# Layer 1's attention on one Trainium2 core: the heads taken two by two, TensorE's order written out

## The chip, the core and the metric

The program runs on one core of a Trainium2 chip, in one launch. The core has TensorE (matrix multiplies, and transposes by a multiply with the identity), VectorE (DVE), ScalarE (ACT), GpSimd (POOL) and SyncE (SP, which here only starts DMA transfers). Each takes its own instructions in order and waits on semaphores for the others. Multiplies write PSUM, of which the program uses eight banks of 128 partitions x 512 fp32; everything else lives in SBUF. The metric is the device time of one execution in microseconds (us), the median over the runs.

## The reference, cut to what matters

Two layers over 256 tokens of width 1024: retention and a dense SwiGLU, then chunked attention and a top-2-of-8 SwiGLU with expert weights of 352 MB. The change is in layer 1's attention: 16 heads of 64 dimensions, each 64-token chunk against its own and the eight chunks before it, with a bias.

```
def one_chunk(args):
    c, q_c = args
    ...
    s = jnp.einsum('bihd,bjhd->bhij', q_c, k_band).astype(jnp.float32) + bias
    ...
    a = jax.nn.softmax(s, axis=-1).astype(v_band.dtype)
    return jnp.einsum('bhij,bjhd->bihd', a, v_band)
o = lax.map(one_chunk, (jnp.arange(nc), q))
...
return o @ w_o
```

## The kernel before

All weights stream from HBM in units of 1 MB. The class `Stream` loads a unit into a raw buffer (SP), and splits it into a high half (a cast on ACT, L157) and a low half (a subtraction on DVE, L158), into a pair of buffers `whi`, `wlo`; five pairs are in rotation from the middle of the attention on. Each product is three multiplies (high by high, high by low, low by high) in fp32r, for which a multiply stands once in the trace. The attention's own small products (scores, transposes, values) are plain fp32, for which each multiply stands twice in the trace, with a weight load each.

In layer 1 the keys `kT` and queries `qT` are kept with 64 dimensions of a head on partitions 0 to 63 (even heads, `par` 0) or 64 to 127 (odd heads, `par` 1). The loop of 19 steps takes one head a step:

- `score(n)`: the scores of head n in one PSUM bank `sc`, two multiplies (256 columns L946, 128 columns L947), each of them 64 rows by 128 columns of the array; then on DVE the bias is added into an SBUF tile `s` and the maxima are taken, and ACT takes the exponentials (L960, L963).
- a piece of filling work for TensorE: in steps 0 to 7 half of a projection `kqps` (24 multiplies of 256 columns), in steps 8 to 17 half a unit of the output projection `y` (`out1`, 6 multiplies of 512 columns, L414 to L418).
- `turn(n-2)`: three transposes into the bank `at` (L974), copied to SBUF by ACT (L977).
- `values(n-3)`: six multiplies into the bank `ao` (L987 to L989; with the odd head four DVE scalings by the sum's reciprocal). Each second step `att_oT` transposes a finished pair (`otr`, L1042), which ACT and DVE split into `ht`, the operand of `out1`.

The banks `sc`, `at`, `ao`, `otr` and `kqps` come from one ring of four; `y` has four of its own. In this loop nothing is ordered by hand: a scheduler places the instructions of each engine, by program order as priority and by readiness in its own plan. Behind the loop the order of TensorE, ACT, DVE and SP is by hand (`order`), through the experts to the end.

Of the kernel before, what the change touches and what calls it, by code (L numbers as in the profile page):

```python
# [9 lines left out]
F32 = mybir.dt.float32  # L10
# [7 lines left out]
P = 128  # L18
T = 256
# [40 lines left out]
PC = 1  # L60
PM = 2
RE = 1
# [21 lines left out]
C_ID, C_TRI, C_IOTA, C_INV, C_DEC = 0, 128, 256, 384, 385  # L84
C_END = C_DEC + HEADS * T
LINE = 16
M = 96
E_X, E_Y, E_END = 0, 8, 64
C_TILE = 400
EDGE = 56  # L90

# [127 lines left out]
def trunk(ctx: ExitStack, tc: tile.TileContext, a, out):  # L219
    nc = tc.nc  # L220
    base = ctx.enter_context(tc.tile_pool(name="base", bufs=1))
# [10 lines left out]

    edge = ctx.enter_context(tc.tile_pool(name="edge", bufs=1, side="right"))
    edge.tile([P, EDGE], F32, name="edge")
    cst = base.tile([P, C_TILE], F32, name="cst")[:, :C_DEC]
    ext = base.tile([P, E_END], F32, name="ext")
    ones = base.tile([P, P], F32, name="ones")
    nhalf = base.tile([P, LINE], F32, name="nhalf")[:, :1]
    wr = base.tile([P, KC, NE], F32, name="wr")
    wrs = base.tile([P, KC, 2 * NE], F32R, name="wrs")  # L240
    gain2 = base.tile([P, 2 * D], F32, name="gain2")
# [60 lines left out]
    st = Stream(nc, units, raws, pairs)  # L302
# [17 lines left out]
    def bank(name):  # L320
        return ring.tile([P, NF], F32, name=name, tag="ring")
# [4 lines left out]
    def t512(name):  # L326
        return tmps[-1].tile([P, NF], F32, name=name, tag="t")

    def s1(name, w=1, dt=F32):
        return small.tile([P, w], dt, name=name, tag=f"s{w}{dt}")  # L330
# [31 lines left out]
    def split_bank(hi, lo, b):  # L362
        nc.scalar.copy(hi, b)  # L363
        nc.vector.tensor_tensor(lo, b, hi.bitcast(F32), op=OP.subtract)  # L364
# [40 lines left out]
    def down(ys, us, xs, first, last, mid=None, at=2):  # L405
        k = 0
        n = sum(u[1][0].shape[1] for u in us)
        for _, (wh, wl) in us:
            for c in range(wh.shape[1]):
                if mid and k == at:  # L410
                    mid()
                for nb in range(2):
                    f = slice(nb * NF, (nb + 1) * NF)
                    nc.tensor.matmul(ys[nb], xs[0][:, k, :], wh[:, c, f], start=first and k == 0, stop=False)  # L414
                    nc.tensor.matmul(ys[nb], xs[0][:, k, :], wl[:, c, f], start=False, stop=False)  # L415
                for nb in range(2):
                    f = slice(nb * NF, (nb + 1) * NF)
                    nc.tensor.matmul(ys[nb], xs[1][:, k, :], wh[:, c, f], start=False, stop=last and k == n - 1)  # L418
                k += 1
# [11 lines left out]
    def hp(n=HP):  # L431
        return tc.high_priority(offset=n) if n else ExitStack()
# [6 lines left out]
    pairs1 = [tuple(pp.tile([P, 1024], F32R, name=f"p{j}{i}") for j in ("hi", "lo")) for i in range(8 - NB)]  # L439
# [73 lines left out]
    def take_ht():  # L513
        x = (htr.popleft(), htr.popleft())
        htr.extend(x)
        return x
# [75 lines left out]
    start = tc.manual_schedule(engines={mybir.EngineType.PE, mybir.EngineType.Activation, mybir.EngineType.DVE})  # L592
# [8 lines left out]
    def norm0(tb):  # L601
        r = s1("rstd")
        nc.vector.tensor_tensor(r, ss[tb][:, 0:1], ss[tb][:, 1:2], op=OP.add)
        nc.vector.tensor_scalar(r, r, 1.0 / D, EPS, op0=OP.mult, op1=OP.add)
        nc.gpsimd.tensor_tensor(r, r, nhalf, op=OP.pow)
        scaled(xh[tb], h[:, tb, :], r, gains[0])
        return [transpose4(xh[tb][:, half * NF : (half + 1) * NF], "xtr") for half in range(2)]
# [4 lines left out]
    b = bank("warm")  # L612
# [4 lines left out]
    bs = norm0(0)  # L617
# [8 lines left out]
    bs = norm0(1)  # L626
# [251 lines left out]
    r3 = ExitStack()  # L878
    stacks.append(r3)
    ap_ = r3.enter_context(tc.tile_pool(name="att", bufs=1))  # L880
    ap3 = r3.enter_context(tc.tile_pool(name="att3", bufs=3))
    vsb = ap_.tile([P, 2, D], F32, name="vsb")
    kT = [ap_.tile([P, 4, T], F32, name=f"kT{i}") for i in range(2)]
    qT = [ap_.tile([P, 4, T], F32, name=f"qT{i}") for i in range(2)]
# [4 lines left out]
    def load_bias(pr):  # L889
        b = bias[pr % 2]  # L890
        nc.sync.dma_start(b[64:128, :, :], a["bias_hi"][:, 2 * pr : 2 * pr + 2, :])
        nc.sync.dma_start(b[0:64, :, :192], a["bias_lo"][:, 2 * pr : 2 * pr + 2, :])
# [44 lines left out]
    class Att:  # L937
        def __init__(self):
            self.s, self.e, self.t = {}, {}, {}

        def score(self, hd):
            half, ch, par = hd // 8, (hd % 8) // 2, hd % 2
            rr = slice(par * 64, par * 64 + 64)
            q, k = qT[half][rr, ch, :], kT[half][rr, ch, :]
            b = bank("sc")
            nc.tensor.matmul(b[:, :T], q[:, P:], k, start=True, stop=True)  # L946
            nc.tensor.matmul(b[:, T : T + P], q[:, :P], k[:, :P], start=True, stop=True)  # L947
            bt = bias[(hd // 2) % 2][:, par, :]
            s = ap3.tile([P, T + P], F32, name="s")
            nc.vector.tensor_tensor(s[:, :T], b[:, :T], bt, op=OP.add)  # L950
            nc.vector.tensor_tensor(s[:, T:], b[:, T : T + P], bt[:, P:], op=OP.add)
            if par == 1 and hd // 2 + 2 < 8:
                load_bias(hd // 2 + 2)
            nm = s1("nm", 2)
            nc.vector.tensor_reduce(nm[:, 0:1], s[:, T:], axis=AX.X, op=OP.max)
            nc.vector.tensor_reduce(nm[:, 1:2], s[:, :T], axis=AX.X, op=OP.max)
            nc.vector.tensor_scalar(nm, nm, -1.0, None, op0=OP.mult)
            if par == 0:
                self.sum = s1("esum", 4)
            nc.scalar.activation(  # L960
                s[:, :T], s[:, :T], AF.Exp, bias=nm[:, 1:2], accum_out=self.sum[:, 2 + par : 3 + par]
            )
            nc.scalar.activation(s[:, T:], s[:, T:], AF.Exp, bias=nm[:, 0:1], accum_out=self.sum[:, par : par + 1])  # L963
            self.s[hd] = s
            if par == 1:
                rs = s1("rsum", 4)
                nc.vector.reciprocal(rs, self.sum)
                self.e[hd // 2] = rs
# [31 lines left out]
    att = Att()  # L1000
# [26 lines left out]
    dst, xo, wo, swapped, late = [], [], {}, [], []  # L1027

    def swap_right():
        p1.close()  # L1030
        mw = m0.enter_context(tc.tile_pool(name="more0", bufs=1, side="right"))
        late.extend(mw.tile([P, 2048], F32, name=f"more{i}") for i in range(6))
        swapped.append(True)

    def att_oT(ch):

        if ch % 2 == 0:
            xo.append(take_ht())
        b = bank("otr")[:, :T].rearrange("p (b t) -> p b t", b=2)
        c = ch % 4 * P  # L1040
        for tb in range(2):
            nc.tensor.transpose(b[:, tb, :], dst[ch // 4][tb][:, c : c + P], ident)  # L1042
        f = slice(ch % 2 * 2, ch % 2 * 2 + 2)
        with hp(H1):
            split_bank(xo[-1][0][:, f, :], xo[-1][1][:, f, :], b)

    def out1(ch, tb, n=99):
        if ch not in wo:
            wo[ch] = st.take1()
        k = ch % 2 * 2 + tb  # L1050
        down(y[tb], wo[ch], [x[:, k : k + 1, :] for x in xo[ch // 2]], ch == 0, ch == 7)
        if tb == 1:
            st.done(wo.pop(ch))
            if not swapped and not st.retired:
                swap_right()
            st.pump1(n)

    fill = proj_fill()
    outs = [(0, 0), (0, 1), (1, 0), (1, 1), (2, 0), (2, 1), (3, 0), (3, 1)] + OV[OO][0]
    for n in range(19):  # L1060
        if n < 16:
            att.score(n)
        if n < 8:
            next(fill, None)
        if n == 8:
            for _ in fill:
                pass
            if not RE:
                st.retire(pairs1)
            elif not st.retired:  # L1070
                swap_right()
        for _ in range(PC if n % PM == 0 else 0):
            if late:
                st.raws.append(late.pop(0))
                st.load()
        if n >= 8 and n < 19 and outs[n - 8]:
            out1(*outs[n - 8])
        if 2 <= n <= 17:
            att.turn(n - 2)
        if n >= 3:  # L1080
            if (n - 3) % 8 == 0:
                dst.append([t512("ao0"), t512("ao1")])
            att.values(n - 3, dst[-1])
        if n >= 5 and n % 2:
            att_oT((n - 5) // 2)
    for x in OV[OO][1]:
        out1(*x)
    att_oT(7)
# [530 lines left out]
    with tc.If(over > M):  # L1619
        with ExitStack() as es:  # L1620
            q = es.enter_context(tc.tile_pool(name="ov", bufs=1))
# [67 lines left out]
```

## Time and profile before

| what | value |
|---|---|
| median of 3 runs | 1562.42 us (1562.37 to 1562.57) |
| the profiled execution | 1563.2 us, of which the span of the instructions is 1561.3 us |
| TensorE | busy 1537.8 us, 98% |
| DVE, ACT | 1275.3 us (82%), 1091.5 us (70%) |
| granted TensorE clock | 0.998 of full speed, which is the upper of its two levels (2.4 GHz) |

The profile is of one execution. A busy TensorE means that some multiply was in its pipeline: a 512-column multiply stands with 0.39 us in the trace, but the next starts 0.23 to 0.24 us behind it. Work on TensorE is therefore read from start to start.

### The profile page before, as it was taken

What the parts mean: (1) busy time and instruction counts of PE and PEld (TensorE: products, weight loads), DVE (VectorE), ACT (ScalarE), POOL (GpSimd) and SP (SyncE); (2) the same over time, 40 slices, a digit from 0 to 9 for tenths busy, and PEclk for the clock granted to TensorE, in tenths of its full rate; (3) what the DMA queues carried; (4) which work ended last, traced back from release to release, by engine and by line L of the source; (5) the groups of instructions that cost most, each with busy time, mean ns of one, the idle gap of its engine ahead of it and who ended that gap; (6) DMA issues with size and microseconds to landing.
All of it is one profiled execution on the core that took longest, in us unless ns stands there. A gap on an engine that the chain in (4) does not pass through costs nothing.

```text
span 1561.3 us, 20789 instructions
## 1 busy us (share of the span) xinstructions
PE 1537.8 (98%) x7556; PEld 1290.6 (83%) x7556; DVE 1275.3 (82%) x1617; ACT 1091.5 (70%) x1461; POOL 48.4 (3%) x67
## 2 busy tenths in 40 slices
PE   7999999999999999999999999999999999999997
PEld 5888888888889888888888888888888888888886
DVE  7866675555774779999999999999999999999995
ACT  6545454554754658888878888888888788788774
POOL 1000010000000001000000000000000000000000
PEclk9999999999999999999999999999999999999999
DMA  8854476555463779999999999999999999999850
GB/s 294 286 180 167 162 254 216 187 188 196 149 217 124 267 269 378 412 391 381 378 382 394 381 373 388 366 382 390 373 386 391 375 368 398 380 369 390 310 211 30
DMA packets 206303, 473.56 MB, mean 303 GB/s; under 512 B 9168, under 2 KB 21328, under 8 KB 206192
## 3 DMA queue, kind: packets, MB, share of 16 engines
q1 hardware_dynamic: 202064, 457.87, 79.8%
q0 software_dynamic: 3840, 13.76, 2.4%
q8 instruction: 61, 1.00, 0.2%
q10 hardware_dynamic: 288, 0.52, 0.1%
q14 instruction: 50, 0.41, 0.1%
HBM read 462.16 MB, written 9.96 MB: 302 GB/s over the span
## 4 chain that ended last, share of the span: by engine, by line
PE 98%; ACT 1%; DVE 0%; DMA 0%; issue 0%; SPq 0%; POOL 0%; ACTq 0%; POOLq 0%; DVEq 0%
PE y L414 9%; PE y L415 9%; PE y L418 9%; PE g L333 8%; PE g L334 8%; PE g L335 8%; PE u L333 8%; PE u L335 8%; PE u L334 8%; PE vps L335 1%; PE vps L333 1%; PE vps L334 1%; PE htr L1230 1%; PE kqps L400 1%; PE qkps L401 1%; PE qkps L402 1%
## 5 line engine op out<-in xcount | busy, mean ns | idle before, releaser
L158 DVE TENSOR_TENSOR wlo<-raw,whi 128x512 fp32r<-128x512 f32 (+1 forms) x414 | 375.0, 929 | 109.5 <-ACT whi L157 94.4
L157 ACT CAST whi<-raw 128x512 fp32r<-128x512 f32 (+1 forms) x414 | 329.0, 812 | 139.0 <-PE y L418 49.7
L158 DVE TENSOR_TENSOR wlo<-more,whi 128x1024 fp32r<-128x1024 f32 (+1 forms) x275 | 327.4, 1214 | 26.4 <-ACT whi L157 14.1
L157 ACT CAST whi<-more 128x1024 fp32r<-128x1024 f32 (+1 forms) x275 | 284.6, 1049 | 58.6 <-PE y L418 29.5
L414 PE MATMUL y<-whi,ht 128*128 128x512 f32 x548 | 216.0, 394 | 0.5 <-ACT ht L363 0.5
L415 PE MATMUL y<-wlo,ht 128*128 128x512 f32 x548 | 213.9, 390 | 0.0
L333 PE MATMUL u<-whi,xd 128*128 128x512 f32 x448 | 180.3, 402 | 0.0
L333 PE MATMUL g<-whi,xd 128*128 128x512 f32 x456 | 177.9, 390 | 0.2 <-ACT xd L363 0.2
L335 PE MATMUL g<-whi,xd 128*128 128x512 f32 x456 | 177.9, 390 | 0.0
L334 PE MATMUL g<-wlo,xd 128*128 128x512 f32 x456 | 177.5, 389 | 0.0
L335 PE MATMUL u<-whi,xd 128*128 128x512 f32 x448 | 175.2, 391 | 0.0
L334 PE MATMUL u<-wlo,xd 128*128 128x512 f32 x448 | 174.5, 389 | 0.0
L418 PE MATMUL y<-whi,ht 128*128 128x512 f32 x548 | 169.0, 390 | 0.0
L414 PEld LDWEIGHTS y<-whi,ht 128*128 128x128 f32 x548 | 102.9, 188 | 21.9 <-ACT ht L363 1.0
L418 PEld LDWEIGHTS y<-whi,ht 128*128 128x128 f32 x548 | 102.9, 188 | 21.8
L415 PEld LDWEIGHTS y<-wlo,ht 128*128 128x128 f32 x548 | 103.0, 188 | 20.8
L158 DVE TENSOR_TENSOR wlo<-mraw,whi 128x1024 fp32r<-128x1024 f32 x91 | 109.3, 1223 | 10.3 <-ACT whi L157 5.1
L157 ACT CAST whi<-mraw 128x1024 fp32r<-128x1024 f32 x91 | 94.7, 1056 | 19.1 <-PE y L418 9.5
L158 DVE TENSOR_TENSOR wlo<-spare,whi 128x1024 fp32r<-128x1024 f32 x84 | 100.6, 1221 | 8.1 <-ACT whi L157 4.3
L335 PEld LDWEIGHTS g<-whi,xd 128*128 128x128 f32 x456 | 85.6, 188 | 18.2 <-DVE xd L364 0.4
L333 PEld LDWEIGHTS g<-whi,xd 128*128 128x128 f32 x456 | 85.6, 188 | 18.1 <-ACT xd L363 0.5
L157 ACT CAST whi<-spare 128x1024 fp32r<-128x1024 f32 x84 | 87.5, 1055 | 18.6 <-PE y L418 9.1
(363 smaller groups left out, 2632.0 us busy)
## 6 DMA issues: line engine op xcount, KB each, us to landing
more<-in_w_gate_moe_dram SPq DMA_DIRECT2D x56, 1024.0 KB, 7.1
more<-in_w_down_moe_dram SPq DMA_DIRECT2D x46, 1024.0 KB, 7.7
raw<-in_w_up_moe_dram SPq DMA_DIRECT2D x45, 1024.0 KB, 7.0
more<-in_w_up_moe_dram SPq DMA_DIRECT2D x35, 1024.0 KB, 7.0
raw<-in_w_gate_moe_dram SPq DMA_DIRECT2D x25, 1024.0 KB, 7.2
raw<-in_w_in_a_dram SPq DMA_DIRECT2D x23, 1024.0 KB, 5.2
raw<-in_w_down_moe_dram SPq DMA_DIRECT2D x22, 1024.0 KB, 7.3
mraw<-in_w_down_moe_dram SPq DMA_DIRECT2D x22, 1024.0 KB, 7.1
```

The costliest lines, as they stand in the source:

```text
L157: self.nc.scalar.copy(hi[:, f], r[:, g])
L158: (lo_engine or self.nc.vector).tensor_tensor(lo[:, f], r[:, g], hi[:, f].bitcast(F32), op=OP.subtract)
L333: nc.tensor.matmul(o, lh, rh, start=start, stop=False)
L334: nc.tensor.matmul(o, lh, rl, start=False, stop=False)
L335: nc.tensor.matmul(o, ll, rh, start=False, stop=stop)
L400: nc.tensor.matmul(o, wh[:, c, f], xh_, start=k == 0, stop=False)
L401: nc.tensor.matmul(o, wh[:, c, f], xl_, start=False, stop=False)
L402: nc.tensor.matmul(o, wl[:, c, f], xh_, start=False, stop=k == KC - 1)
L414: nc.tensor.matmul(ys[nb], xs[0][:, k, :], wh[:, c, f], start=first and k == 0, stop=False)
L415: nc.tensor.matmul(ys[nb], xs[0][:, k, :], wl[:, c, f], start=False, stop=False)
L418: nc.tensor.matmul(ys[nb], xs[1][:, k, :], wh[:, c, f], start=False, stop=last and k == n - 1)
L1230: nc.tensor.transpose(b[:, c, :m], x[:m, c0 + c * P : c0 + (c + 1) * P], ident[:m, :m])
```

## The change: pairs of heads

The loop has nine steps of one pair each. `scores(m)` takes two banks and gives the 256-column multiplies of both heads, then the 128-column ones of both; even and odd head lie in different halves of the partitions. `turn` and `values` of both heads of the pair before follow, with a piece of filling work between each of these blocks (`between`). TensorE's order is the program's within the loop (`by_pairs`); the other engines stay with the scheduler. `s` gets a pool of four buffers instead of three; for that the constant `nhalf` moves into a free column of `cst` and `ext` shrinks from 64 to 16 columns. One switch (`RE`) that was always on is no longer asked.

```
-E_X, E_Y, E_END = 0, 8, 64
+E_X, E_Y, E_END = 0, 8, 16
...
-        def score(self, hd):
-            half, ch, par = hd // 8, (hd % 8) // 2, hd % 2
-            rr = slice(par * 64, par * 64 + 64)
-            q, k = qT[half][rr, ch, :], kT[half][rr, ch, :]
-            b = bank("sc")
-            nc.tensor.matmul(b[:, :T], q[:, P:], k, start=True, stop=True)
-            nc.tensor.matmul(b[:, T : T + P], q[:, :P], k[:, :P], start=True, stop=True)
+        def scores(self, pr):
+
+            half, ch = pr // 4, pr % 4
+            rows2 = [slice(par * 64, par * 64 + 64) for par in range(2)]
+            qk = [(qT[half][rr, ch, :], kT[half][rr, ch, :]) for rr in rows2]
+            bs = [bank("sc") for _ in range(2)]
+            for b, (q, k) in zip(bs, qk):
+                nc.tensor.matmul(b[:, :T], q[:, P:], k, start=True, stop=True)
+            for b, (q, k) in zip(bs, qk):
+                nc.tensor.matmul(b[:, T : T + P], q[:, :P], k[:, :P], start=True, stop=True)
+            for par in range(2):
+                self.exps(2 * pr + par, bs[par])
+
+        def exps(self, hd, b):
+            par = hd % 2
             bt = bias[(hd // 2) % 2][:, par, :]
-            s = ap3.tile([P, T + P], F32, name="s")
+            s = ap4.tile([P, T + P], F32, name="s")
...
+    by_pairs = tc.manual_schedule(engines={mybir.EngineType.PE})
+    by_pairs.__enter__()
+
+    def between(n):
         if n < 8:
             next(fill, None)
...
+        elif outs[n - 8]:
+            out1(*outs[n - 8])
+
+    for m in range(9):
+        if m < 8:
+            att.scores(m)
+        if m == 4:
             for _ in fill:
                 pass
...
+        if late:
+            st.raws.append(late.pop(0))
+            st.load()
+        between(2 * m)
+        if m:
+            att.turn(2 * m - 2)
+            att.turn(2 * m - 1)
+        between(2 * m + 1)
+        if m:
+            if (m - 1) % 4 == 0:
                 dst.append([t512("ao0"), t512("ao1")])
...
+            att.values(2 * m - 2, dst[-1])
+            att.values(2 * m - 1, dst[-1])
+        if m >= 2:
+            att_oT(m - 2)
+    by_pairs.__exit__(None, None, None)
```

Before the change, TensorE's row at head 13 (`sc` scores, `y` output projection, `at` transposes, `ao` values) reads:

```order
L946 MATMUL sc<-kT_3499,qT_3501 128x256
L947 MATMUL sc<-kT_3499,qT_3501 128x128
L414 MATMUL y_3966<-whi_90,ht_108 128x512
L415 MATMUL y_3966<-wlo_91,ht_108 128x512
L414 MATMUL y_3967<-whi_90,ht_108 128x512
L415 MATMUL y_3967<-wlo_91,ht_108 128x512
L418 MATMUL y_3966<-whi_90,ht_109 128x512
L418 MATMUL y_3967<-whi_90,ht_109 128x512
L974 MATMUL at<-cst,s 128x128 x3
L987 MATMUL ao<-vsb,at 128x64
L988 MATMUL ao<-vsb,at 128x64
L989 MATMUL ao<-vsb,at 128x64
```

The next head begins with the same two score multiplies again. With the change, TensorE's row at the pair of heads 12 and 13 reads:

```order
L949 MATMUL sc<-kT_3501,qT_3503 128x256 x2
L951 MATMUL sc<-kT_3501,qT_3503 128x128 x2
L414 MATMUL y_3966<-whi_89,ht_107 128x512
L415 MATMUL y_3966<-wlo_90,ht_107 128x512
L414 MATMUL y_3967<-whi_89,ht_107 128x512
L415 MATMUL y_3967<-wlo_90,ht_107 128x512
L418 MATMUL y_3966<-whi_89,ht_108 128x512
L418 MATMUL y_3967<-whi_89,ht_108 128x512
L983 MATMUL at<-cst,s 128x128 x6
L414 MATMUL y_3968<-whi_89,ht_107 128x512
```

One block of scores stands where two stood, the six transposes are together, and the values (which before came right behind the transposes, for the head before) now come six multiplies `y` behind the transposes of the same heads. Outside the loop TensorE's row is the same before and after.

ACT's row before, from the exponentials of one head to those of the next but one (`s` exponentials, `at` copy of the transposes, `whi` weight cast, `ht` split of `otr`):

```order
L960 ACTIVATE s,esum<-s,nm 128x256
L963 ACTIVATE s,esum<-s,nm 128x128
L977 COPY at<-at 128x384
L960 ACTIVATE s,esum<-s,nm 128x256
L963 ACTIVATE s,esum<-s,nm 128x128
L157 CAST whi_90<-raw_85 128x512
L977 COPY at<-at 128x384
L157 CAST whi_90<-raw_85 128x512
L363 CAST ht_110<-otr 128x256
```

ACT's row with the change, from the copies of one pair to those of the next:

```order
L986 COPY at<-at 128x384 x2
L157 CAST whi_87<-raw_84 128x512
L969 ACTIVATE s,esum<-s,nm 128x256
L972 ACTIVATE s,esum<-s,nm 128x128
L157 CAST whi_87<-raw_84 128x512
L969 ACTIVATE s,esum<-s,nm 128x256
L972 ACTIVATE s,esum<-s,nm 128x128
L363 CAST ht_107<-otr 128x256
L986 COPY at<-at 128x384 x2
```

Both copies of a pair now stand ahead of the exponentials of the pair behind it.

## Rows read from the trace of the kernel before

**Rows 1.** The page: the span, and the chain that ended last by engine.
```profile
span 1561.3 us, 20789 instructions
...
PE 98%; ACT 1%; DVE 0%; DMA 0%; issue 0%; SPq 0%; POOL 0%; ACTq 0%; POOLq 0%; DVEq 0%
```
**Rows 2.** Busy time by stretch (stretch, length, PE, PEld, DVE, ACT, POOL, clock, DMA).
```profile
477.30:514.20 36.90, 36.90 (x278) 34.53 (x277) 19.71 (x65) 19.70 (x56) 0.00 (x0) 1.00 0.25 83
514.20:550.00 35.80, 35.34 (x207) 29.16 (x206) 24.88 (x88) 20.97 (x62) 0.00 (x0) 1.00 0.86 307
580.00:1500.00 920.00, 920.00 (x4220) 761.15 (x4219) 853.86 (x806) 745.67 (x797) 18.50 (x22) 1.00 1.01 379
```
**Rows 3.** Waits, 470 to 550 us (total, times, longest).
```profile
PE y L414 <- ACT ht L363: 0.5, 1, 0.5
```
**Rows 4.** TensorE's multiplies in order of time (start, length), heads 13 to 15.
```profile
530.51 0.49 PE L974 MATMUL at<-cst,s 128*128 128x128 f32 x3
...
531.01 0.39 PE L988 MATMUL ao<-vsb,at 128*128 128x64 f32 x2
531.23 0.39 PE L989 MATMUL ao<-vsb,at 128*128 128x64 f32 x2
531.55 0.70 PE L946 MATMUL sc<-kT,qT 64*128 64x256 f32 x2
532.08 0.38 PE L947 MATMUL sc<-kT,qT 64*128 64x128 f32 x2
532.39 0.50 PE L414 MATMUL y<-whi,ht 128*128 128x512 f32 x1
532.73 0.40 PE L415 MATMUL y<-wlo,ht 128*128 128x512 f32 x1
532.97 0.39 PE L414 MATMUL y<-whi,ht 128*128 128x512 f32 x1
...
538.52 0.70 PE L946 MATMUL sc<-kT,qT 64*128 64x256 f32 x2
```
**Rows 5.** TensorE's weight loads (PEld) in the same stretch.
```profile
531.54 0.29 PEld L946 LDWEIGHTS sc<-kT,qT 64*128 64x128 f32 x2
...
532.39 0.19 PEld L414 LDWEIGHTS y<-whi,ht 128*128 128x128 f32 x1
532.50 0.19 PEld L415 LDWEIGHTS y<-wlo,ht 128*128 128x128 f32 x1
```
**Rows 6.** Layer 0's scores: fp32 multiplies of 128 rows, 180 us.
```profile
179.65 1.02 PE L558 MATMUL sps<-qk,qk 128*128 128x256 f32 x4
180.51 0.61 PE L560 MATMUL sps<-qk,qk 128*128 128x128 f32 x4
```
**Rows 7.** ACT in order of time, heads 13 and 14.
```profile
531.09 0.48 ACT L977 COPY at<-at 128x384 f32<-128x384 f32 x1 [0.73 <-PE at L974]
532.11 0.51 ACT L960 ACTIVATE s<-s,nm 128x256 f32<-128x256 f32 x1 [0.54 <-DVE nm L957]
...
532.91 0.19 ACT L963 ACTIVATION_READ_ACCUMULATOR s<-s,nm 128x1 f32 x1
...
534.47 0.48 ACT L977 COPY at<-at 128x384 f32<-128x384 f32 x1
534.85 0.62 ACT L157 CAST whi<-raw 128x512 fp32r<-128x512 f32 x1
```
**Rows 8.** TensorE behind the loop's last values.
```profile
549.23 0.27 PE L1042 MATMUL otr<-cst,ao 128*128 128x128 f32 x1
549.97 0.50 PE L414 MATMUL y<-whi,ht 128*128 128x512 f32 x1 [0.46 <-ACT ht L363]
```
**Rows 9.** DMA issues, 500 to 600 us (count, KB, us to landing).
```profile
bias<-in_bias_hi_dram SPq DMA_DIRECT2D x4, 128.0 KB, 3.7
```
**Rows 10.** Waits in the experts, 700 to 1000 us.
```profile
ACT whi L157 <- PE y L418: 21.0, 69, 0.3
```
**Rows 11.** Waits of SP's DMA queue, 700 to 1000 us.
```profile
SPq L135 <- DVE wlo L158: 251.3, 107, 3.3
```

More of the change, by code (lines that the diff above doesn't have):

```diff
@@ L234, in trunk @@
     edge.tile([P, EDGE], F32, name="edge")
-    cst = base.tile([P, C_TILE], F32, name="cst")[:, :C_DEC]
+    cst_all = base.tile([P, C_TILE], F32, name="cst")
+    cst, nhalf = cst_all[:, :C_DEC], cst_all[:, C_DEC : C_DEC + 1]
     ext = base.tile([P, E_END], F32, name="ext")
     ones = base.tile([P, P], F32, name="ones")
-    nhalf = base.tile([P, LINE], F32, name="nhalf")[:, :1]
     wr = base.tile([P, KC, NE], F32, name="wr")
@@ L881, in trunk @@
     ap3 = r3.enter_context(tc.tile_pool(name="att3", bufs=3))
+    ap4 = r3.enter_context(tc.tile_pool(name="att4", bufs=4))
     vsb = ap_.tile([P, 2, D], F32, name="vsb")
@@ L1059, in trunk @@
     outs = [(0, 0), (0, 1), (1, 0), (1, 1), (2, 0), (2, 1), (3, 0), (3, 1)] + OV[OO][0]
-    for n in range(19):
-        if n < 16:
-            att.score(n)
+    by_pairs = tc.manual_schedule(engines={mybir.EngineType.PE})
+    by_pairs.__enter__()
+    def between(n):
         if n < 8:
             next(fill, None)
-        if n == 8:
+        elif outs[n - 8]:
[4 more added lines that the diff above has]
+        if m == 4:
             for _ in fill:
                 pass
-            if not RE:
-                st.retire(pairs1)
-            elif not st.retired:
+            if not st.retired:
                 swap_right()
[L1072 to L1081, printed above, removed]
-                dst.append([t512("ao0"), t512("ao1")])
-            att.values(n - 3, dst[-1])
-        if n >= 5 and n % 2:
-            att_oT((n - 5) // 2)
+        if late:
[8 more added lines that the diff above has]
+            if (m - 1) % 4 == 0:
+                dst.append([t512("ao0"), t512("ao1")])
+            att.values(2 * m - 2, dst[-1])
[3 more added lines that the diff above has]
+    by_pairs.__exit__(None, None, None)
     for x in OV[OO][1]:
```

## The prediction

> **What bounds the kernel now.** I read the page first: the chain that ended last is 98% TensorE [rows 1]. So what counts is the time from one TensorE instruction's start to the next, and I went to the stretches. In the loop of the change, 477 to 550 us, TensorE is busy without a break in the first half and but for 0.46 us in the second [rows 2], and the list of waits has one wait of TensorE, 0.5 us for `ht`, which lies behind the last values [rows 3, 8]. DVE is busy 24.88 of 35.80 us in the second half, ACT 20.97: neither is the bound. The experts, 580 to 1500 us, have TensorE busy 920.00 of 920.00 us. A microsecond saved in TensorE's row in the loop is thus a microsecond of the kernel, unless a new wait or a later stage takes it back.
>
> **What a block of scores costs.** Each of a head's two score multiplies stands as two records (x2), so a head has four multiplies and four weight loads, and 16 heads have 64 of each. I follow head 13 through TensorE's row [rows 4], start to start:
> - The last multiply pair of the values starts at 531.23, the scores at 531.55. Two such multiplies take 0.22 (531.01 to 531.23 is the pair before), so 0.10 us is lost ahead of the scores.
> - 531.55 to 532.08 is 0.53 us for two 256-column multiplies, 532.08 to 532.39 is 0.31 us for two of 128 columns.
> - The first `y` behind them takes 0.34 us to the next (532.39 to 532.73), where 0.24 is usual (532.73 to 532.97): 0.10 us lost.
>
> Together 1.04 us. How much of it is streaming? Layer 0's fp32 scores, with all 128 rows, take 0.86 us for four 256-column multiplies (179.65 to 180.51), 0.215 each [rows 6], and by half the columns a 128-column one takes about 0.107. A head is 2 x 0.215 + 2 x 0.107 = 0.64 us. The other 0.40 us is the price of going into the 64-row form and out of it: 0.10 us of standing still on each side (ahead of 531.55, and 0.31 less two times 0.107 ahead of 532.39), and a weight load of 0.11 us with no multiply beside it on each side, since load and multiply start together there (531.54 and 531.55; 532.39 and 532.39) [rows 4, 5].
>
> **What the change makes of it.** The scores of two heads stand together: eight blocks of eight multiplies for sixteen of four. Eight times 0.40 us of going in and out falls away for certain, 3.2 us. The rest depends on whether the multiplies of the even head, on partitions 0 to 63, run beside those of the odd head, on 64 to 127. No row of before has two such multiplies next to each other, so I bound the pair's block:
> - nothing runs side by side: 2 x 0.64 + 0.40 = 1.68 us, against 2.08 for two blocks now: 0.40 saved a pair;
> - all of it does: 0.64 + 0.40 = 1.04 us: 1.04 saved a pair;
> - the multiplies overlap, but the eight weight loads follow each other. Loads stand at least 0.11 us apart in the rows (532.39 to 532.50; the two of the scores fill 0.29 us, which is 0.11 and one load's length) [rows 5]. Eight times 0.11 is 0.88, then the last multiply 0.107, and around it the standing still (0.10 twice) and the `y` load's 0.105: 1.29 us, so 0.79 saved a pair.
>
> I take the third. The two heads share neither partitions nor a bank, which speaks against the first; but the loads never come closer than 0.11 us in these rows, and both passes of a head stand ahead of the other head's in the order, which speaks against the second. The order of starts alone gives about the same: if a multiply may start only once the one before it has started, even heads' second passes run beside odd heads' first, three times 0.215 and twice 0.107, 0.86 us, and 0.40 around it.
>
> Sum: 8 x 0.79 = 6.3 us. The rest of the row is the same work: 24 multiplies of `kqps` or 6 of `y` at a time, six transposes, six values, two `otr`. A pair of heads now takes 6.97 us in the second half (531.55 to 538.52 [rows 4]); it would take 6.18.
>
> **What is costed at nothing, and its cover.** A head's transposes came two head steps behind its scores; a pair's now come one pair step and six `y` behind, about 7.5 us, for the softmax of two heads. DVE does the same work in less time: 24.88 us in 35.80 less 3.2, 76%. ACT's exponentials of a head take 1.0 us (532.11 to 533.10), its copy 0.38 (534.47 to 534.85), a cast 0.62 [rows 7]: for two heads with two casts that is 4.0 us of 6.18. The bias loads stand in SP's queue behind the odd head's additions, which now come after the even head's; they land 3.7 us after the issue [rows 9] and are needed two pair steps, some 12 us, behind the scores that free their buffer. Of the six extra raw buffers five are filled in the loop and the sixth behind it, a weight of the experts that is read much later. At the loop's end the transposes `otr` now stand right in front of the `y` that needs their split, where six `y` stood between; but the last pair's own `otr` is then covered by that `y`. Now TensorE loses 0.63 us there (549.23 and 0.11 to 549.97 [rows 8]); by the same path (transposes, ACT's cast, the load) it loses 0.6 us at the other `y`, so I put nothing. The smaller `ext`, the moved `nhalf` and the fourth `s` change no instruction's count.
>
> The profiled execution took 1563.2 us, 1.9 us more than its span, and 0.8 more than the median. It would become 1556.9; the median 1562.42 becomes **1556.1 us**. This kernel's measurement tells a change from none at about 0.2%, 3.1 us.
>
> **The rivals.**
> - Nothing runs side by side: 8 x 0.40 = 3.2 us, 1559.2, on the edge of what can be told. For it: every multiply in these rows waits for the one before it to stream. Against it: no row puts two different halves next to each other.
> - All runs side by side: 8 x 1.04 = 8.3 us, 1554.1. For it: halves and banks are apart. Against it: loads 0.11 us apart, and the order. The Trainium skill, "TensorE: Matmul & The Clock Gate", Part 3, on packing small matmuls, says that multiplies on different row groups run at once, some 4 ns apart, with their loads overlapped; by it this would be the time. No run here shows it yet.
> - Values wait for copies, and the kernel gets slower. Copies used to have a whole head step, now they have six `y`. The first copy can start 0.58 us behind its transposes (530.51 to 531.09 [rows 4, 7]) and is done 0.48 later, at 1.06; the values come six transposes of 0.11 and six `y` of 0.23 behind, at 2.05: 0.99 us to spare. It decides in the five steps of the second half (in the first, 24 `kqps` stand there, twice as long). If the exponentials of both heads and two casts, 3.2 us, were ahead of the copies, each step would lose 2.25: 11.3 in all, 1567.4. The kernel becomes measurably slower from 1.9 us of loss a step, so from copies 2.9 us late. Against it: ACT's order has the copies ahead of the exponentials of the next pair. A lateness of 1.5 us would lose 2.6 us: 1558.7.
> - The experts give it back: 1562.4. If the splitting of weights or the DMA set their pace, TensorE would only wait there. Against it: ACT's casts wait for TensorE to free a pair, 69 times in 300 us for 0.3 us each [rows 10], and SP's loads wait for DVE to free a raw buffer [rows 11]. TensorE sets the pace, and what is behind it waits for it.
>
> **How the numbers follow.** The third kind of block 0.42, all side by side 0.15, nothing 0.24, copies late by a little 0.07 (1558 to 1561), copies late enough to be slower 0.05, given back 0.07. The range takes the blocks between their bounds with half a microsecond of room (1553.6) and reaches over the small lateness to 1560.8; outside stay the given-back, the slower and a bit of the lateness, 0.15. Faster by over 0.2% (below 1559.3): the first two, over half of the third, and part of the fourth, 0.73. Within 0.2%: the rest of these and the given-back, 0.22. Slower: 0.05.
>
> **What will show it.** Between the first score multiply of a pair and the first multiply behind the block stands about 1.09 us (third case), 0.84 (all) or 1.48 (none); where heads overlap, the odd head's multiply starts before the even head's has streamed 0.215 us. TensorE's list of waits in the loop should have no `ao` behind ACT's `at`; the experts should still show 920 busy in 920 us. I am wrong if the block is 1.48 us or more, if values wait, or if TensorE begins to wait in the experts.

## The result and the profile after

The changed kernel takes 1554.58 us, the median of 5 runs (1553.83 to 1554.92), against 1562.44 of before on the same chip (1562.37 to 1562.9): a ratio of 0.9949, with an interval of 0.9938 to 0.9960, or 7.9 us less. The prediction was 1556.1, with a range of 1553.6 to 1560.8. The profiled execution took 1553.83 us with a span of 1552.1 and a granted clock of 0.998, as before. The time is inside the range, and 1.5 us lower than the number: what happened is the rival in which all of a pair's multiplies run side by side, for which 1554.1 had been worked out and a chance of 0.15 given.

The page of the changed kernel, its span and its chain by engine, beside [rows 1]:

```profile
span 1552.1 us, 20782 instructions
...
PE 98%; ACT 1%; DVE 0%; DMA 0%; issue 0%; SPq 0%; POOL 0%; ACTq 0%; POOLq 0%; DVEq 0%
```

Busy time by stretch (columns as in [rows 2]); the loop now lies between 476 and 539 us:

```profile
476.00:510.00 34.00, 34.00 (x288) 32.67 (x288) 20.28 (x68) 20.70 (x58) 0.00 (x0) 1.00 0.29 94
510.00:548.00 38.00, 37.54 (x233) 31.76 (x232) 28.26 (x94) 22.25 (x67) 0.55 (x1) 1.00 0.73 259
580.00:1500.00 920.00, 920.00 (x4223) 761.34 (x4222) 854.27 (x797) 745.69 (x797) 16.32 (x21) 1.00 1.01 379
```

TensorE is still without a break in the first half and, but for 0.46 us, in the second, and the experts still have 920.00 of 920.00. So the gain was not won by filling idle time: TensorE has a shorter row. Its list of waits, 470 to 550 us, has the wait for `ht` as before [rows 3], a short one behind the loop, and nothing else:

```profile
PE y L414 <- ACT ht L363: 0.5, 1, 0.5
PE g L333 <- ACT xd L363: 0.2, 1, 0.2
```

TensorE's multiplies in order of time, from the scores of one pair to those of the next, beside [rows 4]:

```profile
515.43 0.39 PE L1051 MATMUL otr<-cst,ao 128*128 128x128 f32 x2
515.75 0.70 PE L949 MATMUL sc<-kT,qT 64*128 64x256 f32 x4
516.28 0.39 PE L951 MATMUL sc<-kT,qT 64*128 64x128 f32 x4
516.60 0.50 PE L414 MATMUL y<-whi,ht 128*128 128x512 f32 x1
516.93 0.39 PE L415 MATMUL y<-wlo,ht 128*128 128x512 f32 x1
517.16 0.40 PE L414 MATMUL y<-whi,ht 128*128 128x512 f32 x1
...
521.75 0.49 PE L949 MATMUL sc<-kT,qT 64*128 64x256 f32 x2
```

Each score line now counts four multiplies, two of each head, and yet is as long as the line of two in [rows 4]: 515.75 to 516.28 is 0.53 us, and 516.28 to 516.60 is 0.32. From the first score to the first `y` it is 0.85 us. Around it stand the same losses as before: 0.10 ahead (515.43 to 515.75 is 0.32, and two such transposes take 0.22), and 0.10 behind (516.60 to 516.93 is 0.33, the next takes 0.23). That makes 1.05 us for two heads, where two blocks took 2.08: 1.03 saved a pair, 8.2 in eight. The step from pair to pair is 6.00 us, where it was 6.97: 0.97 less. Of the 1.03, 0.05 goes back at the values, which both heads now give in one go: in the single records their twelve take 1.28 us (526.127 to 527.409), where a head's six took 0.62 before (534.215 to 534.832).

The weight loads of the same block, beside [rows 5]:

```profile
515.74 0.30 PEld L949 LDWEIGHTS sc<-kT,qT 64*128 64x128 f32 x4 [0.17 <-DVE wlo L158]
516.07 0.41 PEld L951 LDWEIGHTS sc<-kT,qT 64*128 64x128 f32 x4
516.60 0.19 PEld L414 LDWEIGHTS y<-whi,ht 128*128 128x128 f32 x1
```

Four loads fill 0.30 us, where two filled 0.29. The single records of the block before this one (509.75 us) show why: the even head's first load and multiply start at 509.751 and 509.752, the odd head's at 509.757 and 509.759; the second products start at 510.072 and 510.079. The odd head is 6 or 7 ns behind in all 32 pairs of multiplies of the loop, and its loads are 6 or 7 ns behind too.

The loop as a whole can be measured better than the kernel, since it leaves out the rest of the run. Counted from the first score multiply to the first of the experts' transposes `xrt` behind it, it took 79.62 us (477.29 to 556.91) and now takes 71.42 (476.31 to 547.73): 8.20 less. That is eight times 1.03; the 0.05 a pair at the values must be made up by shifts as small elsewhere in the loop, which were not followed. The spans differ by 9.2; the other 1.0 us lies ahead of the loop, in code that the change does not touch, and the start of the loop scatters by as much in the profiles of the other kernels (476.1 to 477.5). Behind the loop nothing is given back: from that first `xrt` to the end it is 1004.4 us before and 1004.3 after.

### The profile page after: what moved, and what is told of

Same layout as the page of the kernel before. It is cut to its first block, busy times and chain, and to the rows that moved or that the text cites. A ratio compares the mean times of both kernels' runs of the same rounds, so it can differ in the third digit from the quotient of the medians.

```text
span 1552.1 us, 20782 instructions
## 1 busy us (share of the span) xinstructions
PE 1528.8 (98%) x7556; PEld 1284.1 (83%) x7556; DVE 1274.0 (82%) x1617; ACT 1089.7 (70%) x1461; POOL 47.9 (3%) x67
## 4 chain that ended last, share of the span: by engine, by line
PE 98%; ACT 1%; DVE 0%; DMA 0%; issue 0%; SPq 0%; POOL 0%; ACTq 0%; POOLq 0%; DVEq 0%
PE y L414 9%; PE y L415 9%; PE y L418 9%; PE g L333 8%; PE g L335 8%; PE g L334 8%; PE u L333 8%; PE u L335 8%; PE u L334 8%; PE vps L335 1%; PE vps L334 1%; PE vps L333 1%; PE htr L1246 1%; PE kqps L400 1%; PE qkps L402 1%; PE qkps L401 1%
```

## The experiments

The theory after the result: (a) eight blocks less save what going into the 64-row form and out of it costs, 0.40 us each, 3.2 us; (b) the halves run side by side, loads included, 0.64 us a pair, 5.1 us; (c) all else is covered. Beside the experiments the kernel before took 1562.65 to 1562.83 us. Each experiment's ratio is to that, and "the loop" is counted as above (where an expectation has 71.2 for the change, it counts to the first weight load of `xrt`, 0.23 us earlier).

**The halves in the order of the heads.** Both products of the even head stand ahead of both of the odd head:

```
             for b, (q, k) in zip(bs, qk):
                 nc.tensor.matmul(b[:, :T], q[:, P:], k, start=True, stop=True)
-            for b, (q, k) in zip(bs, qk):
                 nc.tensor.matmul(b[:, T : T + P], q[:, :P], k[:, :P], start=True, stop=True)
```

> The pair's four score products in another order: both of the even head, then both of the odd head, still one block in two banks. Theory A (a product may start only once the one before it in the order has started; the halves run side by side when that allows it): the odd head's 256-column product starts with the even head's 128-column one, 0.43 us into the block, and streaming takes 1.07 us instead of 0.64; each of eight blocks is 0.43 us longer than with the change, 3.4 us in all, about 1558.0 us. Theory B (each half works through its own products, whatever their order in the row): no difference to the change, 1554.6 us, and the odd head's first product starts some 0.01 us behind the even head's.

Measured: 1555.01 us (1553.84 to 1555.38), ratio 0.9951 [0.9937, 0.9964]; the loop 71.47. TensorE's multiplies of the block:

```profile
509.53 0.71 PE L949 MATMUL sc<-kT,qT 64*128 64x256 f32 x4
510.07 0.39 PE L950 MATMUL sc<-kT,qT 64*128 64x128 f32 x4
510.39 0.50 PE L414 MATMUL y<-whi,ht 128*128 128x512 f32 x1
```

The odd head's first multiply is now the fifth of the row, and the list still shows it in the first group: in the single records it starts at 509.543, 13 ns behind the first (509.530), and 0.31 us ahead of the even head's second (509.850), which stands ahead of it in the program. (The trace does not name the head. But the four 256-column multiplies have all started by 509.863, and the first 128-column one, the even head's and third in the row, starts at 510.066. And where both heads lie in one half, as in the next experiment, a second pass starts 0.32 us behind the first and not 13 ns.) Each half works through its own products; with four multiplies and their loads ahead of it in the row the odd head lags by 13 or 14 ns, with two by 6 or 7. So the order of the row within a block does not matter, and the prediction's second argument against full overlap, the order of starts, falls as well.

**Both heads on one half.** Both heads take partitions 0 to 63; all else is the change:

```
-            rows2 = [slice(par * 64, par * 64 + 64) for par in range(2)]
+            rows2 = [slice(0, 64) for par in range(2)]
```

> Scores of both heads of a pair are taken from the even head's keys and queries, so the odd heads' scores are replaced by the even heads': the same instructions in the same order, but all on partitions 0 to 63. Theory (the gain is 3.2 us from eight blocks less and 5.1 us from the two halves side by side): the second part falls away, each block streams 1.28 us instead of 0.64, the kernel is 5.1 us slower than with the change, about 1559.7, and still 2.7 us faster than before. Rival (the gain is from grouping and order, not from the halves): about 1554.6, as with the change.

Measured: 1559.61 us (1559.02 to 1560.77), ratio 0.9981 [0.9972, 0.9990]; the loop 76.55, 5.13 more than the change and 3.07 less than before. TensorE's multiplies of the block:

```profile
512.32 1.13 PE L949 MATMUL sc<-kT,qT 64*128 64x256 f32 x4
513.28 0.60 PE L951 MATMUL sc<-kT,qT 64*128 64x128 f32 x4
513.82 0.50 PE L414 MATMUL y<-whi,ht 128*128 128x512 f32 x1
```

1.50 us from the first score to `y` for 0.85: 0.65 a pair, which is one head's streaming. This divides the gain: of 8.20 us in the loop 5.1 come from the halves side by side, and 3.1 from the rest of the change, for which eight blocks instead of sixteen were to give 3.2.

**The block cut in two.** The first piece of filling work goes between the 256-column and the 128-column products, so that there are sixteen blocks again, each with both halves:

```
             for b, (q, k) in zip(bs, qk):
                 nc.tensor.matmul(b[:, :T], q[:, P:], k, start=True, stop=True)
+            mid()
             for b, (q, k) in zip(bs, qk):
...
+        def mid():
...
+            between(2 * m)
```

> The changed kernel with the first piece of filling work of a pair put between its 256-column and its 128-column score multiplies: sixteen blocks of scores again in place of eight, the same multiplies, and the two heads still next to each other in each block. Theory (0.40 us is the price of going into the 64-row form and out of it, once for each block, and the two halves run side by side in a block of any length): eight blocks more cost 8 x 0.40 = 3.2 us, the loop from the first scores to the experts' transposes 74.4 us for 71.2, the time 1557.8. Rival (the price belongs to each multiply or each head, and the number of blocks is not what counts; the gain beyond the streaming came from the new order of the other work): the loop stays within 0.5 us of 71.2, the time 1554.6. A third possibility, told by a wait of TensorE on `s`: the later 128-column scores make the softmax late.

Measured: 1559.41 us (1558.32 to 1560.17), ratio 0.9979 [0.9970, 0.9988]; the loop 76.04, 4.62 more than the change, where 3.2 had been expected. TensorE's multiplies of one step, first its two blocks of scores:

```profile
513.74 0.70 PE L949 MATMUL sc<-kT,qT 64*128 64x256 f32 x4
514.37 0.50 PE L414 MATMUL y<-whi,ht 128*128 128x512 f32 x1
...
515.42 0.62 PE L418 MATMUL y<-whi,ht 128*128 128x512 f32 x2
515.97 0.49 PE L952 MATMUL sc<-kT,qT 64*128 64x128 f32 x4
516.39 0.87 PE L984 MATMUL at<-cst,s 128*128 128x128 f32 x6
517.02 0.48 PE L414 MATMUL y<-whi,ht 128*128 128x512 f32 x1
...
518.03 0.62 PE L418 MATMUL y<-whi,ht 128*128 128x512 f32 x2
518.49 0.33 PE L997 MATMUL ao<-vsb,at 128*128 128x64 f32 x2
...
520.09 0.73 PE L949 MATMUL sc<-kT,qT 64*128 64x256 f32 x4
```

This step waits for nothing and takes 6.35 us for 6.00 (513.74 to 520.09): 0.35 for one block more, 2.8 us in eight. A block's price is thus confirmed, a little below the 0.40. Coming out, 0.10 us of standing still is lost as before (515.97 to 516.39 is 0.42, for a load of 0.11 and two times 0.107 of streaming), but then the transposes take only 0.06 more (516.39 to 517.02 is 0.63, where the change has 0.57), where `y` takes 0.10 more: 0.16 in place of 0.2. The price is not a wait for another engine: the second block's loads wait for no semaphore in the trace, and still the two `y` ahead of it take 0.55 us (515.42 to 515.97). Two ahead of the values, which are plain fp32 too but of 128 rows, take 0.46 (518.03 to 518.49); so it is the 64 rows that cost, and not the change from fp32r to fp32.

The other 1.8 us are waits, as in the third possibility of the expectation, but not for the softmax. The list of TensorE's waits in the loop:

```profile
PE at L984 <- DVE s L961: 0.7, 3, 0.2
PE y L414 <- ACT ht L363: 0.5, 1, 0.5
...
PE at L984 <- DVE ao L1006: 0.2, 1, 0.2
```

L961 is DVE's addition of the 128-column scores of the pair in work, and the transposes read the pair before: the only thing that links them is a bank. The two `sc`, a `kqps` and the first `at` are the ring of four, and the second head's transposes come only when the additions have read the scores. The list counts 0.2 us for each, because the modelled ends of multiplies cover part of it; from start to start the six transposes take 1.08 us in these three steps (488.67 to 489.75, the first), for 0.57: 1.5 in all. The wait for `ao`, DVE's scalings of the values, which the transposes do not read either, costs 0.3 from start to start in one step (522.33 to 523.04 is 0.71, for 0.42). The change does not meet that, since a whole piece of filling work lies between its scores and its transposes.

**The hand order alone, and its absence.** The change without the hand order of TensorE (the two lines of `by_pairs` and the one that ends it left out), and the kernel before with such an order around its own loop:

```
-    by_pairs = tc.manual_schedule(engines={mybir.EngineType.PE})
-    by_pairs.__enter__()
...
-    by_pairs.__exit__(None, None, None)
```

> The change without TensorE's order by hand; the scheduler places the loop. Its row comes out nearly the same: the pair's products together, one multiply of y moved once, and the end of the loop. Theory (the pairs give the gain): within 0.6 us of the change, 1554.0 to 1555.2. Rival (the hand order gives a part of it): over 1 us slower than the change, 1555.6 or more.

> The kernel before, one head a step, with TensorE's order by hand in its loop. Theory (the pairs give the gain): as before, 1562.4 within 0.6 us, since TensorE's work and its going in and out of the 64-row form stay (16 blocks). Rival (the order gives a part): over 1 us faster than before, 1561.4 or less.

Measured: 1554.57 us (1553.79 to 1555.09), ratio 0.9947 [0.9934, 0.9961], the loop 71.40; and 1562.75 (1561.98 to 1563.42), ratio 1.0 [0.9991, 1.0009], the loop 79.81. The order by hand gives nothing that can be told from zero; the pairs give it all.

**The values at once.** The second piece of filling work goes behind the values (and behind `otr`), so that the values come right behind the transposes:

```
             att.turn(2 * m - 1)
-        between(2 * m + 1)
         if m:
...
         if m >= 2:
             att_oT(m - 2)
+        between(2 * m + 1)
```

> The changed kernel with the second piece of filling work moved behind the values, so that the six values of a pair come right behind its six transposes; the filling work that covers ACT's two copies is gone. Theory (the six multiplies of y are what hides the copies): the copies begin about 0.6 us behind the first transposes and the first is done 0.48 later, at 1.06 us, while the values could start at 0.65 us; TensorE waits some 0.4 us for the first copy in each of eight steps, and little for the second: about 3.3 us slower than the change, 1558, with waits of the values on `at` behind ACT in the list. Rival (the copies are in time anyway, the place of the filling work does not matter): no such wait, 1554.6 as the change.

Measured: 1560.92 us (1560.36 to 1561.33), ratio 0.9988 [0.9979, 0.9997]; the loop 77.53, 6.1 more than the change, where 3.3 had been expected. The wait exists, and is larger. TensorE's list of waits, then its row, then ACT's, at one step:

```profile
PE ao L996 <- ACT at L986: 4.1, 11, 1.0
```

```profile
522.16 0.82 PE L983 MATMUL at<-cst,s 128*128 128x128 f32 x6
523.27 0.43 PE L996 MATMUL ao<-vsb,at 128*128 128x64 f32 x2 [0.30 <-ACT at L986]
...
523.77 0.39 PE L998 MATMUL ao<-vsb,at 128*128 128x64 f32 x2
524.52 0.43 PE L996 MATMUL ao<-vsb,at 128*128 128x64 f32 x2 [0.36 <-ACT at L986]
```

```profile
522.74 0.48 ACT L986 COPY at<-at 128x384 f32<-128x384 f32 x1 [1.92 <-PE at L983]
523.12 0.51 ACT L969 ACTIVATE s<-s,nm 128x256 f32<-128x256 f32 x1
...
524.00 0.46 ACT L986 COPY at<-at 128x384 f32<-128x384 f32 x1
```

The first copy is about as estimated: the values start 1.11 us behind the transposes, for 0.57 when covered, 0.54 lost. What the expectation put at little is the second head: here ACT takes a head's exponentials between the two copies, so the second copy ends 1.2 us after the first (524.46 for 523.22), and the second three values come 0.75 us behind the one before them (523.77 to 524.52) where 0.22 is usual: another 0.53. Not every step is like this one. In the single records the second copy is this late in three of the eight steps; in one (514.91) both copies stand behind a head's exponentials and the values come 1.80 us behind the transposes; in the other four only the first copy is waited for, some 0.5 us. (The list of waits has 4.1 us in all, since it counts only from the modelled end of the multiply before; the loop lost 6.1. The wait of 0.5 us for `ht` is gone from the list, since the filling work now stands behind `otr`; so the 6.1 is what is left after that gain.) The cover is worth 6 us or a little more, and the filling of the change hides all of it: in its list of waits no `ao` stands behind `at`.

**The two transposes `otr` earlier**, right behind the transposes of the next pair:

```
             att.turn(2 * m - 1)
+        if m >= 2:
+            att_oT(m - 2)
         between(2 * m + 1)
...
-        if m >= 2:
-            att_oT(m - 2)
```

> The changed kernel with the two transposes `otr` of a finished pair moved ahead of the second piece of filling work, right behind the transposes of the next pair, so that six multiplies of y and six values stand between them and the y that reads their split. Theory (TensorE stands still 0.5 us once at the loop's end for `ht`, and nowhere else in the loop): that wait goes and nothing else changes, 0.5 to 0.6 us faster than the change, 1554.0, too little to be told in the medians but seen in the list of waits and as a loop shorter by that much. Rival (the split is late for another reason, ACT's queue): the wait stays, and the loop keeps its 71.4 us.

Measured: 1554.95 us (1554.48 to 1555.56), ratio 0.9951 [0.9938, 0.9965]; the loop 71.79, 0.37 more than the change. TensorE's list of waits, 470 to 550 us:

```profile
PE otr L1051 <- ACT at L986: 0.3, 1, 0.3
PE g L333 <- ACT xd L363: 0.2, 1, 0.2
PE y L414 <- ACT ht L363: 0.2, 1, 0.2
```

The wait of 0.5 us for `ht` did shrink to 0.2 (what is left is the last pair's own, which stands closer to its `y`); but in one step `otr` now waits 0.3 us for ACT's copy of `at`. It reads nothing of that copy; that it waits for a bank of the ring is likely, but no row names the bank. That step takes 6.51 us (515.87 to 522.38), the next 5.99. Neither theory is right: the stall of the end gets shorter, and a new one comes for it. The place where the change has these transposes is as good.

**Three buffers for `s`.**

```
-    ap4 = r3.enter_context(tc.tile_pool(name="att4", bufs=4))
+    ap4 = r3.enter_context(tc.tile_pool(name="att4", bufs=3))
```

> The changed kernel with three buffers `s` for the score rows in place of four. The second head of a pair then waits for a buffer until the transposes of the pair before have read it, so its additions on DVE begin later. Theory (the softmax of two heads has about 2 us to spare ahead of its transposes, TensorE does not wait for `s`): the time stays at that of the change, 1554.6 within 1 us. Rival (the softmax sets the pace as soon as one buffer is missing): TensorE's transposes wait for `s`, 0.5 us or more a step, 1558 or more.

Measured: 1554.15 us (1553.44 to 1554.31), ratio 0.9944 [0.9931, 0.9958]; the loop 71.41. DVE waits for the buffer (its waits in the loop, one row of the list):

```profile
DVE s L959 <- PE at L983: 6.1, 3, 2.1
```

In the change this row does not exist. Three times some 2 us late on DVE, and no wait of TensorE: the softmax has that much to spare in its pair step. The fourth buffer, and the moved constant and the smaller `ext` that make room for it, give no time here.

## Why the prediction was right, and where its number was off

- **TensorE's row is the bound, and what is cut from it is gained.** Right: 8.20 us less in the loop, no new wait there, and the experts keep 920 of 920, so nothing is given back: behind the loop the time is the same within 0.1 us.
- **Eight blocks less, 3.2 us.** Right: 3.07 in the loop with both heads on one half, small shifts elsewhere included, and by the cut block 2.8 at a place where coming out is cheaper.
- **"I take the third", the eight weight loads 0.11 us apart.** This step failed. A pair's block was put at 1.29 us and a saving of 0.79; it is 1.05 and 1.03. Eight times 0.24 is 1.9 us, which is the difference in the loop (8.2 for 6.3); in the medians the number was 1.5 us off. That the time lies in the range does not bear this step out: the range held because it reached to the bound at which all runs side by side, and what happened had been given 0.15, against 0.42 for the step that was taken. The 0.11 us is right as a distance between loads that follow each other in one half or in all rows; it was carried over to loads into different halves, which no row of before showed. These start 6 or 7 ns apart, load and multiply alike. The Trainium skill, "TensorE: Matmul & The Clock Gate", Part 3, The mechanism, has multiplies on different row groups (here the two halves) start some 4 ns apart, with loads that overlap running multiplies. By this trace that is so, with 6 or 7 ns.
- **The order of starts as a limit, 0.86 us of streaming.** Wrong too: later products of the other half are not held back by the order. The change's own trace has it already, where the odd head's first multiply, third in the row, starts at 509.759 and the second at 510.072; the experiment with the heads in order shows it with the multiply fifth. The same section of the Trainium skill says that multiplies start in the order of the program. Here one that stands fifth starts 0.31 us ahead of the second, and the measurement decides.
- **The covers.** Copies, exponentials, bias loads and DVE's work stayed hidden, as costed. For the copies that was shown by taking the cover away (6.1 us), for the softmax by delaying it (2 us late, no wait). "0.99 us to spare" for the first copy came out as worked out: in the single records of the step at 512.10 the copy is done 1.06 us behind the first transpose, and the values come at 2.05. The second copy, which had not been worked out, is done at 1.45 and its values come at 2.66: 1.2 to spare.
- **The loop's end.** Costed at nothing, since 0.6 us would be lost at the other `y`, and so it is:

```profile
538.36 0.39 PE L1051 MATMUL otr<-cst,ao 128*128 128x128 f32 x2
539.21 0.50 PE L414 MATMUL y<-whi,ht 128*128 128x512 f32 x1 [0.46 <-ACT ht L363]
539.54 0.27 PE L1051 MATMUL otr<-cst,ao 128*128 128x128 f32 x1
```

The two transposes take 0.22 us from 538.36, and `y` comes at 539.21: 0.63 us lost, as at 549.97 [rows 8]. The last pair's `otr` (539.54) is covered by that `y`.

## What to carry to other kernels

Multiplies with 64 rows cost more than their streaming, 0.40 us a block for entering and leaving between 128-row work here, so put them together; and if two lie on different halves of the partitions, the second was free here (0.85 us from the first score to `y` for two heads, 0.84 for one). Check what the filling work between a product and its reader hides before moving it: taking it away cost 6 us here, though the first wait that it covers was 0.5 us a step. Where a row has no example of two things side by side, a distance measured between things in series is a bound for it, and no more likely than the other end.

## What had not been expected of the hardware

- The two halves pass each other freely: with the heads in order the odd head's first multiply, fifth in the row, starts 13 ns behind the first, and the block takes 0.86 us, as with the change (0.85).
- Coming out of the 64-row form costs about 0.2 us into `y` (0.10 of standing still, 0.10 of an exposed load) and about 0.16 into transposes (0.10 and 0.06), so that a whole extra block ahead of transposes costs 0.35, not 0.40.
